# A hybrid RWKV-7 and short-convolution block on one core: a later issue time for the store of the solved diagonal blocks, an earlier priority for the Gram masks and the weights' casts

## The chip, the core and the metric

The kernel runs on one core of a Trainium2 chip. The metric is the device time of one execution in microseconds (us). Three executions of the kernel before took 1057.23, 1058.88 and 1059.51 us; their median, 1058.88 us, is the number that the change is measured against. Engines are named as in the profile: PE is the matrix engine (PEld its weight loads), DVE, ACT and POOL are the vector, scalar and GpSimd engines, and SP is the queue from which nearly all DMAs are issued.

## What is computed

One layer of a streaming encoder: 16 meta tokens and 512 tokens, width 2048, are normalised and multiplied by one input matrix with 8320 columns. Half of the columns feed 16 heads of RWKV-7 time mixing, the other half a gated convolution of width 3. Both results pass one output projection, are added to the residual and are normalised. Cut to what matters here:

```python
hn = _rmsnorm(h_res, norm_in_g); P = hn @ w_in          # columns: r, k, v, g, low rank | B, C, h, gate
# per head, per token:  sa = S kk;  S = S*w - sa b^T + v k^T;  y = S r
y = _rwkv7_recurrence(r, decay, k, v, kk, kk * a)
y_a = (groupnorm(y) + bonus) * silu(g_r)
y_b = Bg * _causal_depthwise_conv(Cg * hc, conv_w) * silu(g_c)
out = _rmsnorm(h_res + concat([y_a, y_b]) @ w_out)
```

## The kernel before

**Projection.** The input weights come in tiles of 128 columns of the matrix ("units": `k2`, `r2`, `v2`, `g2` and so on, in the order of `plan`, lines 105 to 110). A unit is two loads of 512 KB, `wr<j>` (L134), with j counted over the whole stream. Each load is cut into two quarters of 512 columns, and each quarter is split in two float32r parts: ACT copies it to `wh` (L126), and DVE (first quarter of a load) or POOL (second quarter) subtracts to get `wl` (L127). PE then runs three products per step: `wh` with `xh`, `wh` with `xl`, `wl` with `xh` (L315). There are three raw buffers for `wr` and six for each of `wh` and `wl`; a load is issued when both quarters of the load three places earlier are split.

**Recurrence in chunks of 64 tokens.** For every pair of heads i (0 to 7), `prepare(i)` (L569) makes decayed keys and queries on DVE and ACT; PE forms Gram matrices of them (L625) and DVE masks these into `gt` (`masked`, L632 to L639). There are two Gram passes for each i. The second one reuses the PSUM banks of the first: chunk 8 takes the banks of `zc`, the 16 transposes of the keys (L654) take those of `za`, so PE can't begin it before the masks of the first pass have been read out. The masked matrices then go to DRAM (`sg`, L688; `opd`, L567), the 16 by 16 diagonal blocks come back as `d` (L696), and DVE inverts them by doubling (L700 to L733) into `y`. Then

- `sx <- y` (L748) stores the solved blocks, and `load_inverse` (L737) reads them back as `xT` and `xo` in the layout of heads (four DMAs, L739 and L740);
- `y` has one buffer: POOL's clearing of `y` for the next i (L699) waits until that store has read it.

`invert` (L771) takes two such i at a time (0 and 1, 2 and 3, 4 and 5, 6 and 7); it begins with a transpose of `xT` (L784). After all pairs comes `recur`, and then the output projection (L1069).

**What sets the order.** PE's instructions stand in the order in which the program lists them: the projection is a generator, and `fill(ns)` puts about that many ns of it between two steps of the recurrence. DVE, ACT, POOL and SP are ordered by a scheduler from priorities, and each then works strictly through its own list. `tc.high_priority(offset)` moves instructions forward in priority: `AHEAD` is used for results that PE waits for, `WEIGHTS` for the casts of the weights. `later(ns, fn)` (L482) puts a DMA off until that much projection time has been listed, and `run_pending` (L486) then lists it behind the last weight load:

```python
def run_pending(upto):
    while pending and pending[0][0] <= upto:
        fn = pending.pop(0)[1]
        with tc.issue_after(state["dma"]):
            fn()
```

Of the kernel before, what the change touches and what calls it, by code (L numbers as in the profile page):

```python
# [13 lines left out]
ALU = mybir.AluOpType  # L14
# [4 lines left out]
P = 128  # L19
# [26 lines left out]
)  # L46


AHEAD, WEIGHTS = 3000, 1500


def _constants():
# [24 lines left out]
def hymba_kernel(ctx: ExitStack, tc: tile.TileContext, xt, xtok, w_in, w_out, pv, lup, cst, msk, gf, out):  # L77
    nc = tc.nc
# [11 lines left out]
    gmask = cs[:, C_GM : C_GM + 256].rearrange("p (h c) -> p h c", h=2)  # L90
# [6 lines left out]
    def col(off, i=0):  # L97
        return pvt[:, off + i : off + i + 1]
# [183 lines left out]
    for b in range(2):  # L282
# [5 lines left out]
        out=omm, in0=pvt[:, V_MU : V_MU + 33], scalar1=-1.0, scalar2=1.0, op0=ALU.mult, op1=ALU.add  # L288
    )
    for d, off in (  # L290
# [4 lines left out]
            out=d, in0=pvt[:, off : off + 8], scalar1=0.5, scalar2=None, op0=ALU.mult  # L295
        )
    nc.vector.tensor_scalar(
        out=hv[:, 4], in0=pvt[:, V_KA : V_KA + 8], scalar1=-0.5, scalar2=1.0, op0=ALU.mult, op1=ALU.add
# [183 lines left out]
    def later(ns, fn):  # L482
        pending.append((clock[0] + ns, fn))
        pending.sort(key=lambda e: e[0])
# [48 lines left out]
    def ahead():  # L533
        return tc.high_priority(offset=AHEAD)

    def c3(t):
        return t.rearrange("p (c s) -> p c s", s=CH)
# [31 lines left out]
    def prepare(i):  # L569
        p = i % 2  # L570
# [21 lines left out]
            out=bk[:, :, 0], in0=c3(k), scalar=hv[:, 2, i : i + 1], in1=c3(te), op0=ALU.mult, op1=ALU.mult  # L592
# [3 lines left out]
            out=ta, in0=ta, scalar1=hv[:, 3, i : i + 1], scalar2=hv[:, 4, i : i + 1], op0=ALU.mult, op1=ALU.add  # L596
        )
        nc.vector.scalar_tensor_tensor(
            out=ar[:, :, 0], in0=c3(k), scalar=col(V_KK, i), in1=e1[:, :, 0:CH], op0=ALU.mult, op1=ALU.mult
# [8 lines left out]
            out=ar[:, 1:NCH, 1], in0=c3(r), in1=e1[:, 1:NCH, 1 : CH + 1], op=ALU.mult  # L608
        )
        nc.vector.scalar_tensor_tensor(  # L610
            out=r, in0=r, scalar=hv[:, 5, i : i + 1], in1=ta[:, CH:LP], op0=ALU.mult, op1=ALU.mult
# [8 lines left out]
        gt = cq.tile([P, 2, NCH, P], F32, tag=f"gt{p}", name=f"gt{i}")  # L620
# [9 lines left out]
                )  # L630

        def masked(z, c0, c1):  # L632
            for h in range(2):
                nc.vector.tensor_tensor(
                    out=gt[:, h, c0:c1],
                    in0=z[h],
                    in1=gmask[:, h].unsqueeze(1).to_broadcast([P, c1 - c0, P]),
                    op=ALU.mult,
                )  # L639


        za = [pz.tile([P, 4, P], F32, tag="tz", name=f"g{i}_0_{h}") for h in range(2)]
# [1 line left out]
        for c in range(8):  # L644
            gram(za if c < 4 else zc, c, c // 4 * 4)
        masked(za, 0, 4)
        masked(zc, 4, 8)
        fill(FW["gram2"])
        ze = [pi.tile([P, 1, P], F32, tag=("misc", "ser")[h], name=f"g{i}_8_{h}") for h in range(2)]
        zz = [pz.tile([P, NCH - 1, CH], F32, tag="tz", name=f"bt{i}_{h}") for h in range(2)]  # L650
        gram(ze, 8, 8)
        for c in range(NCH - 1):
            for h, hs, ho in heads:
                nc.tensor.transpose(  # L654
                    zz[h][:, c], bk[hs, c, h : h + 2, :].rearrange("p a s -> p (a s)"),
                    ident[hs, 64 * h : 64 * h + 64],
                )
        masked(ze, 8, 9)
        for h in range(2):
            nc.scalar.copy(bt[:, h], zz[h])  # L660
        fill(FW["gram3"])
        n2 = tr(f"n2{i}")
        for j, (a, b) in enumerate(((0, 288), (288, LP))):
            z = pi.tile([2, b - a], F32, tag=("misc", "ser")[j], name=f"n2_{i}_{a}")
# [11 lines left out]
        sx = scr_x[i % 2]  # L676
# [4 lines left out]
        def blocks(t):  # L681
            return bass.AP(tensor=t.tensor, offset=t.offset, ap=[[BLK, 8 * NCH], [CH, 16], [1, 16]])
# [15 lines left out]
        y = cq.tile([NB, 256], F32, tag="y", name=f"y{i}").rearrange("p (s t) -> p s t", t=16)  # L698
# [11 lines left out]
        def sub(x, r0, c0, dims):  # L710
            return bass.AP(tensor=x.tensor, offset=x.offset + r0 * 16 + c0, ap=[list(x.ap[0])] + dims)

        for m in (2, 4, 8):
            for b in range(16 // (2 * m)):
# [4 lines left out]
                    out=pq,  # L719
                    in0=sub(d, o, o + m, [[16, m], [0, m], [1, m]]),  # L720
                    in1=sub(y, o + m, o + m, [[0, m], [1, m], [16, m]]),
                    op=ALU.mult,
                )
                nc.vector.tensor_reduce(
                    out=tq.rearrange("p (i j) -> p i j", i=m), in_=pq, op=ALU.add, axis=AX.X
                )
                nc.vector.tensor_tensor(
                    out=pq,
                    in0=sub(y, o, o, [[16, m], [0, m], [1, m]]),
                    in1=bass.AP(tensor=tq.tensor, offset=tq.offset, ap=[list(tq.ap[0]), [0, m], [1, m], [m, m]]),  # L730
                    op=ALU.mult,
# [13 lines left out]
                    ),  # L745
                )

        later(12500, lambda: nc.sync.dma_start(blocks(sx), y))  # L748
        later(15500, load_inverse)

        for h, hs, ho in heads:
            stash(i, bt[hs, h], O_B, CH, 64 * h, 64, 0, NCH - 1)
# [241 lines left out]
    for i in range(0, NPAIR, 2):  # L994
        invert([prepare(i), prepare(i + 1)])
# [160 lines left out]
    with tc.manual_schedule(engines={mybir.EngineType.DVE, mybir.EngineType.Activation, mybir.EngineType.Pool}):  # L1156
# [9 lines left out]
        for part in range(2):  # L1166
# [3 lines left out]
            if part == 0:  # L1170
                finish(2)
                nc.vector.tensor_tensor(
                    out=fv[:, 3, 0:1], in0=fv[:, 3, 0:1], in1=ssq[:, 3, 3:4], op=ALU.add
# [60 lines left out]
```

## Time and profile before

| | us |
|---|---|
| executions, median of 3 (lowest to highest) | 1058.88 (1057.23 to 1059.51) |
| profiled execution | 1061.95 |
| its span, first to last instruction | 1060.1 |
| time of PE matmuls within the span | 1039.8 (98%) |
| DVE / ACT / POOL busy | 560.8 / 365.4 / 305.0 |

The profiled execution is 3.07 us above the median of the others, and 1.85 us of it lie outside the span. Matmuls are pipelined and the profile models their ends, so a row's duration (0.28 us for 128x258) is longer than the distance from one start to the next (0.12 us); waits are best read from starts. In a timeline each row is start, duration, engine, line, operation, out<-in, shape and count, and in brackets the idle time before it with what ended it. In a list of waits a row is who waited for whom, then the total, the number of times and the longest, in us. In a table of windows, a row is a stretch of time, its length, the busy time of each engine, the granted clock of PE (1.00 is full speed), the mean share of the DMA engines and GB/s.

### The profile page before, as it was taken

To read this page: it belongs to the slowest core of one execution; us is meant where nothing else is said; L and a number is where in the kernel's file an instruction comes from. 1 tells how busy PE (TensorE), PEld (TensorE's weight loads), DVE (VectorE), ACT (ScalarE), POOL (GpSimd) and SP (SyncE) were. 2 spreads that over 40 slices of the span, in tenths; PEclk is the share of its full clock that TensorE was granted. 3 is DMA by queue.
4 is the path that set the end of the run, shared out by engine and by line. 5 is a ranking of instruction groups with operands and counts; after the bars stand their busy time and mean duration, and the time that the engine had idled before them with its cause. 6 is when DMAs were issued, how large, how long until landed. Compare 5 with 4: busy or idle time off the path is not lost.

```text
span 1060.1 us, 23983 instructions
## 1 busy us (share of the span) xinstructions
PE 1039.8 (98%) x9973; PEld 948.8 (89%) x9973; DVE 560.8 (53%) x1072; ACT 365.4 (34%) x682; POOL 305.0 (29%) x315
## 2 busy tenths in 40 slices
PE   8999999999999999999999999999999999999996
PEld 6999997999998999998999989888798988888885
DVE  6774865558563657563767643354544672212132
ACT  6553422433332433233443332222222342323232
POOL 0132413323232323132332231322323241424232
PEclk9999999999999999999999999999999999999999
DMA  8446474464843364654366648777653879223324
GB/s 290 139 121 158 115 177 141 111 151 105 223 134 115 110 164 115 167 150 117 102 150 157 137 150 275 244 210 239 190 151 90 273 222 331 85 94 100 100 60 159
DMA packets 182893, 167.49 MB, mean 158 GB/s; under 512 B 120960, under 2 KB 143232, under 8 KB 182400
## 3 DMA queue, kind: packets, MB, share of 16 engines
q1 hardware_dynamic: 182208, 164.90, 54.0%
q8 instruction: 78, 1.28, 0.5%
q10 hardware_dynamic: 576, 1.07, 0.3%
q14 instruction: 31, 0.25, 0.1%
HBM read 129.05 MB, written 36.88 MB: 157 GB/s over the span
## 4 chain that ended last, share of the span: by engine, by line
PE 86%; DVE 6%; DMA 3%; issue 2%; POOL 2%; ACT 1%; SPq 0%; DVEq 0%; ACTq 0%; POOLq 0%
PE o L1069 17%; PE ps_C L315 9%; PE ps_gc L315 9%; PE ps_k L315 9%; PE ps_B L315 8%; PE ps_h L315 8%; PE ps_g L315 6%; PE ps_r L315 6%; PE ps_v L315 6%; DMA wr<-in_w_in_dram 2%; PE zs L940 1%; PE g L625 1%; DMA wq<-in_w_in_dram 1%; PE ps_lora L315 1%; PE rz L888 1%
## 5 line engine op out<-in xcount | busy, mean ns | idle before, releaser
L127 POOL TENSOR_TENSOR wl<-wr,wh 128x512 fp32r<-128x512 f32 x150 | 207.7, 1385 | 470.2 <-ACT wh L126 440.7
L126 ACT CAST wh<-wr 128x512 fp32r<-128x512 f32 x312 | 188.7, 619 | 391.6 <-PE o L1069 94.0
L127 DVE TENSOR_TENSOR wl<-wr,wh 128x512 fp32r<-128x512 f32 x162 | 126.1, 783 | 250.9 <-ACT wh L126 240.9
L1069 PE MATMUL o<-wh,m 128*128 128x512 f32 (+1 forms) x484 | 145.3, 384 | 0.0
L1069 PEld LDWEIGHTS o<-wh,m 128*128 128x128 f32 x484 | 89.6, 188 | 21.3
L1069 PE MATMUL o<-wl,m 128*128 128x512 f32 (+1 forms) x242 | 92.6, 389 | 0.0
L315 PE MATMUL ps_g<-xh,wl 128*128 128x258 f32 (+1 forms) x256 | 72.9, 285 | 0.9 <-DVE wl L127 0.8
L315 PE MATMUL ps_h<-xh,wl 128*128 128x258 f32 (+1 forms) x256 | 73.6, 288 | 0.0
L315 PE MATMUL ps_g<-xl,wh 128*128 128x258 f32 (+1 forms) x256 | 73.2, 286 | 0.0
L315 PE MATMUL ps_k<-xl,wh 128*128 128x264 f32 x256 | 73.1, 286 | 0.0
L315 PE MATMUL ps_v<-xh,wh 128*128 128x264 f32 x256 | 73.1, 286 | 0.0
L315 PE MATMUL ps_g<-xh,wh 128*128 128x258 f32 (+1 forms) x256 | 73.0, 285 | 0.0
L315 PE MATMUL ps_h<-xh,wh 128*128 128x258 f32 (+1 forms) x256 | 73.0, 285 | 0.0
L315 PE MATMUL ps_k<-xh,wh 128*128 128x264 f32 x256 | 72.9, 285 | 0.0
L315 PE MATMUL ps_h<-xl,wh 128*128 128x258 f32 (+1 forms) x256 | 72.8, 284 | 0.0
L315 PE MATMUL ps_k<-xh,wl 128*128 128x264 f32 x256 | 72.7, 284 | 0.0
L315 PE MATMUL ps_r<-xh,wh 128*128 128x258 f32 (+1 forms) x256 | 72.2, 282 | 0.5 <-ACT wh L225 0.5
L315 PE MATMUL ps_v<-xh,wl 128*128 128x264 f32 x256 | 72.7, 284 | 0.0
L315 PE MATMUL ps_v<-xl,wh 128*128 128x264 f32 x256 | 72.7, 284 | 0.0
L315 PE MATMUL ps_C<-xh,wh 128*128 128x258 f32 (+1 forms) x256 | 72.3, 282 | 0.0
L315 PE MATMUL ps_C<-xh,wl 128*128 128x258 f32 (+1 forms) x256 | 72.3, 282 | 0.0
L315 PE MATMUL ps_r<-xl,wh 128*128 128x258 f32 (+1 forms) x256 | 72.1, 282 | 0.0
(271 smaller groups left out, 2705.3 us busy)
## 6 DMA issues: line engine op xcount, KB each, us to landing
wr<-in_w_in_dram SPq DMA_DIRECT2D x127, 512.0 KB
ct<-opd SPq DMA_DIRECT2D x64, 288.0 KB
wr<-in_w_out_dram SPq DMA_DIRECT2D x32, 512.0 KB
opd<-ar SPq DMA_DIRECT2D x8, 576.0 KB
opd<-gt SPq DMA_DIRECT2D x16, 288.0 KB
opd<-bt SPq DMA_DIRECT2D x32, 128.0 KB
xres<-in_xtok_dram SPq DMA_DIRECT2D x4, 768.0 KB
out_dram<-xres SPq DMA_DIRECT2D x6, 512.0 KB
```

Source lines behind the costliest of these rows:

```text
L126: nc.scalar.copy(hi, rq)
L127: eng.tensor_tensor(out=lo, in0=rq, in1=hi.bitcast(F32), op=ALU.subtract)
L315: nc.tensor.matmul(ps[r], ww[:, w], xx[:, kt, a:b], start=(kt == 0 and n == 0), stop=(kt == KT - 1 and n == 2))
L625: nc.tensor.matmul(z[h][:, c - c0], bk[hs, c, h : h + 2, :].rearrange("p a s -> p (a s)"), ar[hs, c].rearrange("p a s -> p (a s)"), start= ...
L888: nc.tensor.matmul(z[e][ho if e else hs, 0, k], t[hs, o : o + CH], t[hs, O_V : O_V + CH] if part else st[hs, 4 * e + k], start=(part == 0 ...
L940: nc.tensor.matmul(d[hs, j], t[hs, o : o + CH], x[hs], start=(a == 0), stop=(a == b - 1))
L1069: nc.tensor.matmul(ps[t + p], mm[:, tk], ww[:, o], start=(jj == 0 and q == 0), stop=(jj == KT - 1 and q == 2))
```

## The change

Three edits. The store `sx <- y` and its read-back are put off by more projection time (p is i % 2); the masks of the Gram matrices get the priority of `AHEAD`; and both priority offsets are doubled.

```diff
-AHEAD, WEIGHTS = 3000, 1500
+AHEAD, WEIGHTS = 6000, 3000
...
         def masked(z, c0, c1):
-            for h in range(2):
-                nc.vector.tensor_tensor(
-                    out=gt[:, h, c0:c1],
-                    in0=z[h],
-                    in1=gmask[:, h].unsqueeze(1).to_broadcast([P, c1 - c0, P]),
-                    op=ALU.mult,
-                )
+            with ahead():
+                for h in range(2):
+                    nc.vector.tensor_tensor(
+                        out=gt[:, h, c0:c1],
+                        in0=z[h],
+                        in1=gmask[:, h].unsqueeze(1).to_broadcast([P, c1 - c0, P]),
+                        op=ALU.mult,
+                    )
...
-        later(12500, lambda: nc.sync.dma_start(blocks(sx), y))
-        later(15500, load_inverse)
+        later(13500 if p else 29000, lambda: nc.sync.dma_start(blocks(sx), y))
+        later(16500 if p else 33000, load_inverse)
```

What the two built programs' lists show, engine by engine, for the whole kernel:

- PE and ACT: the same instructions in the same order.
- DVE: the masks stand where they stood. In i = 3, 5 and 7 one split of a weight quarter (`wl80`, `wl128`, `wl176`) changes places with the second half of the PSUM read-out `pr_v` (L334). Nothing else moves.
- POOL: in i = 3, 5 and 7 the clearing of `y` moves behind two weight splits.
- SP, i = 2, 4 and 6 (the one that is solved while its partner is prepared): see the lists below for i = 2; 4 and 6 are the same with other numbers.
- SP, i = 0: the store of the gate `gated0` moves in front of the four read-backs. SP, odd i: nothing moves.

```
SP before: wr39, sx<-y2, wr40, wr41, xT2 xo2 xT2 xo2, wr42, wr43, opd<-ar3, opd<-vs3, wr44, ...
SP after:  wr39, wr40, opd<-ar3, wr41, wr42, sx<-y2, wr43, opd<-vs3, xT2 xo2 xT2 xo2, wr44, ...
```

## The prediction

> **What bounds the kernel now.** I read the page first, then who PE waited for.
>
> ```profile
> span 1060.1 us, 23983 instructions
> PE 1039.8 (98%) x9973; PEld 948.8 (89%) x9973; DVE 560.8 (53%) x1072; ACT 365.4 (34%) x682; POOL 305.0 (29%) x315
> ```
>
> PE is busy for 1039.8 of 1060.1 us and the change leaves its list of instructions alone. So nothing can be won but the waits between PE's instructions, and there are few. The list of PE's waits, its largest rows outside the first 25 us:
>
> ```profile
> PE rz L940 <- issue: 2.0, 1, 2.0
> PE g L625 <- DVE gt L634: 1.5, 3, 0.9
> PE ps_B L315 <- DVE wl L127: 1.4, 1, 1.4
> PE ps_g L315 <- DVE wl L127: 0.8, 2, 0.4
> ```
>
> The second row names what this change is about: three times the second Gram pass (L625) waits for DVE's masks (L634). These are i = 3, 5 and 7. The true price is read from starts in PE's timeline: from the last projection matmul before that pass to the first one after it. First i = 1, where nothing waits, then 3, 5 and 7.
>
> ```profile
> 128.31 0.28 PE L315 MATMUL ps_C<-xh,wl 128*128 128x258 f32 x1
> ...
> 129.44 0.39 PE L315 MATMUL ps_C<-xh,wh 128*128 128x258 f32 x1
> ```
> ```profile
> 267.93 0.28 PE L315 MATMUL ps_g<-xh,wl 128*128 128x256 f32 x1
> ...
> 269.90 0.39 PE L315 MATMUL ps_g<-xh,wh 128*128 128x256 f32 x1
> ```
> ```profile
> 421.60 0.28 PE L315 MATMUL ps_g<-xh,wl 128*128 128x256 f32 x1
> ...
> 424.32 0.39 PE L315 MATMUL ps_g<-xh,wh 128*128 128x256 f32 x1
> ```
> ```profile
> 577.08 0.28 PE L315 MATMUL ps_g<-xh,wl 128*128 128x256 f32 x1
> ...
> 579.24 0.39 PE L315 MATMUL ps_g<-xh,wh 128*128 128x256 f32 x1
> ```
>
> The same work takes 1.13 us at i = 1, and 1.97, 2.72 and 2.16 us at i = 3, 5 and 7 (the last three fences, in this order). The excess is 0.84 + 1.59 + 1.03 = **3.46 us**. That is the whole sum which the masks can give back.
>
> Why are the masks late? The chain of waits, cut to the stretch around i = 5:
>
> ```profile
> 413.18 6.34 DMA wr<-in_w_in_dram
> ...
> 419.62 0.63 ACT wh L126
> ...
> 420.27 0.69 DVE wl L127
> 420.97 2.40 DVE gt L634 x4
> ```
>
> The masks stand behind a weight split (`wl130`, of the load `wr65`) in DVE's list, and that load took 6.34 us to land. The whole chain has the same link for the other two:
>
> ```profile
> 259.52 5.58 DMA wr<-in_w_in_dram
> ```
> ```profile
> 568.74 5.70 DMA wr<-in_w_in_dram
> ```
>
> Why did it take so long? SP's list of waits, and SP's timeline:
>
> ```profile
> SPq L748 <- DVE y L733: 73.3, 6, 16.4
> ```
> ```profile
> 410.24 0.32 SPq L748 DMA_DIRECT2D sx<-y  x1
> 410.65 0.60 SPq L134 DMA_DIRECT2D wr<-in_w_in_dram  x1
> ```
> ```profile
> 413.62 0.60 SPq L739 DMA_DIRECT2D xT<-sx  x1
> ```
>
> SP stood still, up to 16.4 us, until DVE had solved `y4`. Everything behind the store was then issued in a bunch: `wr64` at 410.65, `wr65` at 413.18 (the chain's row), four read-backs from 413.62. `wr65` shared the DMA engines with all of them.
>
> **The change, part by part.**
>
> *The masks' priority: nothing.* DVE's built list has the masks where they were, still behind `wl130`. No instruction is added or removed on any engine. The doubled offsets move only one split past half a PSUM read-out in i = 3, 5 and 7, and nothing on ACT. The wait `ps_g <- wl`, 0.8 us, should therefore stay: the casts it needs stand on ACT behind this row, which waits for DVE.
>
> ```profile
> 408.52 0.62 ACT L551 CAST rk_h<-r 128x512 fp32r<-128x512 f32 x1 [3.80 <-DVE r L610]
> ```
>
> *The later store: this is the working part.* For i = 2, 4 and 6 SP now issues `wr40`, the store of `ar3` (`opd<-ar`), `wr41` and `wr42` ahead of `sx <- y2` (numbers of i = 2). I follow i = 4, where they are `wr64`, `ar5`, `wr65`, `wr66`, `y4`.
>
> ```profile
> 393.68 1.28 POOL L127 TENSOR_TENSOR wl<-wr,wh 128x512 fp32r<-128x512 f32 x1 [0.33 <-ACT wh L126]
> ```
> ```profile
> 410.26 2.90 POOL L127 TENSOR_TENSOR wl<-wr,wh 128x512 fp32r<-128x512 f32 x1 [2.85 <-ACT wh L126]
> ```
> ```profile
> 406.49 0.68 DVE L607 TENSOR_TENSOR ar<-r,e 128x512 f32<-128x512 f32 x1
> ```
> ```profile
> 414.99 1.14 ACT L126 CAST wh<-wr 128x512 fp32r<-128x512 f32 x2 [3.77 <-DMA wr<-in_w_in_dram]
> ```
>
> 1. `wr64` needs the buffer that POOL's split frees at 393.68 + 1.28 = 394.96. It goes out there, some 15.7 us earlier than 410.65.
> 2. `opd<-ar` waits for DVE until 406.49 + 0.68 = 407.17. It holds `wr65` behind it, which costs nothing: `wr65` needs the buffer of `wr62`, which POOL's split frees only at 410.26 + 2.90 = 413.16. So `wr65` is still issued at about 413.2, 6.0 us after `ar5` is ready.
> 3. What changes is its company. `wr64` and `ar5` have landed; `wr66` and the store follow behind it; the read-backs come later still. For its time to landing I take `wr64` of the trace before, the nearest row: issued at 410.65, its cast starts at 414.99, so 4.34 us, with another load 2.5 us behind it. The other end is 6.34, as slow as before.
> 4. At 4.34 us the cast starts at 417.52 instead of 419.62, 2.10 us earlier. ACT and DVE are free by then, since the casts of `wr64`, for which `sh_v` and the rest of `v5` had waited, are no longer late. So the masks come 2.10 us earlier too; they end at 420.97 + 2.40 - 2.10 = 421.27, before PE leaves the projection at 421.60. PE lost 1.59 us there: the wait is gone, with 0.5 us to spare. For i = 3 and 7 the load took 5.58 and 5.70; on the same footing the masks come 1.3 and 1.5 us earlier, against 0.84 and 1.03 us lost, and again about 0.5 us is left.
>
> So the point of decision is a landing time of about 4.8 us: below it the three excesses vanish, at 6.3 none does.
>
> *What else moves, at nothing.* POOL's clearing of `y` now waits for a store that lands later, but stands behind two splits; the split behind it is for a weight quarter that PE reaches more than one unit later (a unit is 96 matmuls of 0.12 us, 11.5 us). If that cover were gone, PE would wait for `wl` as at `ps_B`, 1.4 us. The four read-backs are listed behind `opd<-vs` and land a few us later; `invert` of that pair comes only behind the odd i and another 22.5 us of projection (`fill(FW["solve"])`). `gated0` at i = 0 passes four read-backs that wait for the store anyway. The odd i keep their order. Bounds for each: 0 to 1.4 us lost, and I take 0.
>
> *Sum.* 1061.95 - 3.46 = 1058.49 on the profiled execution's scale; that execution lies 3.07 above the median, so the median comes to 1058.88 - 3.46 = **1055.4 us**.
>
> **A rule against the row: the clock.** The table of windows, at `ps_B` and at i = 5:
>
> ```profile
> 158.51:161.92 3.41, 1.97 (x9) 1.30 (x8) 3.41 (x3) 1.98 (x4) 3.41 (x4) 1.00 0.28 44
> ```
> ```profile
> 161.92:165.33 3.41, 3.41 (x17) 2.75 (x16) 2.24 (x3) 0.62 (x1) 1.46 (x1) 1.00 0.96 254
> ```
> ```profile
> 421.34:424.75 3.41, 2.36 (x28) 1.90 (x27) 2.58 (x6) 0.37 (x1) 0.79 (x1) 1.00 1.07 359
> 424.75:428.17 3.42, 3.42 (x18) 3.42 (x17) 1.12 (x2) 1.26 (x3) 0.16 (x1) 0.50 1.11 308
> ```
>
> Behind the longest of the three waits PE ran for 3.42 us at half clock: 18 matmuls, where 0.12 us each would allow 28. That cost between 10 x 0.12 = 1.2 and half of 3.42 = 1.7 us; I take 1.5. Behind `ps_B`, with less PE work in the window, the clock stayed at 1.00.
>
> The Trainium skill, page "TensorE: Matmul & The Clock Gate", section "HAM oscillation — how this bites in real kernels", gives as its rule that PE should have no idle gap above about 3.4 us. By it a gap of 0.9 us costs no clock, and removing it would give the 3.46 us alone; the row at 424.75 speaks against that, the one at 161.92 for it.
>
> **Rivals.**
>
> - *The half clock goes too.* If the executions that are timed have this stretch as the profiled one has, its 1.5 us go with the wait: 1058.88 - 4.96 = 1053.9. For it: the row. Against: it followed one wait of several, and the median may not hold it.
> - *The change doesn't do what it says.* The masks did not move in DVE's list, so all hangs on one landing time. If `wr65` still takes 5 to 6 us, because `wr66` and the store are now close behind it, PE waits as before: 1058.9. For it: loads in company took 5.58 to 6.34. Against: `wr64` also had a load close behind and took 4.34.
> - *A new wait on SP (slower).* The store, and with it the read-backs and `wr44`, go out later and push the stores of the odd partner's matrices. Before, SP still waited for ACT there, at least this long (i = 7):
>
> ```profile
> SPq L684 <- ACT n L667: 0.8, 1, 0.8
> ```
>
> A delay of SP above 0.8 us moves the odd solve on DVE, and what stands behind it there, by as much. Its price is that of `ps_B`, where weight splits queued behind the solve of i = 1: 1.4 us each in three pairs, 4.2. With the masks' gain that is 1058.88 - 3.46 + 4.2 = 1059.6; with a half clock behind one of them 1061.1, behind all three 1064.1; from one on it counts as slower. How late SP will be, the trace before can't show: the four read-backs, 0.60 us each to issue, move behind `opd<-vs`, 2.4 us, while two weight loads and `opd<-ar` move out of the way ahead of it. It may come out on either side of 0.8.
>
> **How the numbers follow.** The full gain without the clock 0.50 (1055.4); with the clock 0.19 (1053.9); nothing 0.15 (1058.9); the new wait 0.16 (1059.6 to 1064.1). The range takes in the first three with 0.7 us of scatter: 1053.2 to 1059.6. About 0.2%, 2.1 us, is what a measurement of this kernel can tell from no change; that is below 1056.8 or above 1061.0. Faster: 0.47 of the first case, all of the second: 0.66. Slower: the part of the new wait that has a half clock, 0.12. Within: the rest, 0.22.
>
> **What would show it.** Right: PE's waits have no row `g <- gt`; the passages at i = 3, 5 and 7 take 1.13 us; SP's wait `L748 <- y` loses some 45 us and `L567 <- ar` gains most of them; `ps_g <- wl` stays near 0.8; no half clock around i = 5. Wrong: a load in front of the masks still takes over 4.8 us, `wl` waits appear at i = 4 to 7 in the stretch of `invert`, or the gain is smaller than the excess that vanished, which would mean that PE gives it back later.

## The result and the profile after

| | us |
|---|---|
| before, median (lowest to highest) | 1058.2 (1056.29 to 1062.32) |
| after, median (lowest to highest) | 1055.59 (1054.37 to 1059.71) |
| ratio, 95% interval | 0.9976, 0.9966 to 0.9986 |
| after, profiled execution / its span | 1055.68 / 1053.9 |

After is 2.5 us faster by the ratio (1.5 to 3.6); 3.46 was forecast. The same program, timed twice more below (e1, e5), gave 0.9995 and 0.9983. All three together, weighted by their intervals, say 0.9984 or about 1.6 us. e1 alone can't be told from no change, and it lies further from the first timing than their intervals make likely. So a gain is probable, and it is smaller than the first figure.

The page's head and the list of PE's waits, of after:

```profile
span 1053.9 us, 23986 instructions
PE 1035.8 (98%) x9973; PEld 945.8 (90%) x9973; DVE 565.4 (54%) x1072; ACT 366.3 (35%) x682; POOL 307.8 (29%) x315
```
```profile
PE rz L941 <- issue: 1.6, 1, 1.6
...
PE zy L945 <- issue: 1.3, 1, 1.3
...
PE ps_B L315 <- DVE wl L127: 0.9, 1, 0.9
...
PE ps_g L315 <- DVE wl L127: 0.8, 2, 0.4
```

The row `g <- gt` is gone from the list. But a list by releaser shows only waits that the profile can assign. The starts in PE's timeline show that a part of the wait is still there at i = 3 and 5 (first and second pair of rows), and nothing at i = 7:

```profile
266.97 0.28 PE L315 MATMUL ps_g<-xh,wl 128*128 128x256 f32 x1
...
268.43 0.39 PE L315 MATMUL ps_g<-xh,wh 128*128 128x256 f32 x1
...
420.14 0.28 PE L315 MATMUL ps_g<-xh,wl 128*128 128x256 f32 x1
...
421.71 0.38 PE L315 MATMUL ps_g<-xh,wh 128*128 128x256 f32 x1
...
573.11 0.28 PE L315 MATMUL ps_g<-xh,wl 128*128 128x256 f32 x1
...
574.25 0.38 PE L315 MATMUL ps_g<-xh,wh 128*128 128x256 f32 x1
```

The passages take 1.46, 1.57 and 1.13 us, so 0.33 + 0.44 = 0.77 us is left of the 3.46, in this execution. Why? Three views of after around i = 5: POOL, SP (`wr65`, then the moved store), then ACT and DVE.

```profile
408.80 3.85 POOL L127 TENSOR_TENSOR wl<-wr,wh 128x512 fp32r<-128x512 f32 x1 [2.85 <-ACT wh L126]
```
```profile
412.67 0.33 SPq L134 DMA_DIRECT2D wr<-in_w_in_dram  x1
414.27 0.39 SPq L749 DMA_DIRECT2D sx<-y  x1
```
```profile
417.01 0.62 ACT L126 CAST wh<-wr 128x512 fp32r<-128x512 f32 x1 [4.34 <-DMA wr<-in_w_in_dram]
```
```profile
410.82 0.68 DVE L127 TENSOR_TENSOR wl<-wr,wh 128x512 fp32r<-128x512 f32 x1
...
417.66 0.69 DVE L127 TENSOR_TENSOR wl<-wr,wh 128x512 fp32r<-128x512 f32 x1 [1.20 <-ACT wh L126]
418.27 2.89 DVE L635 TENSOR_TENSOR gt<-g,cs 128x512 f32<-128x512 f32 x5
```

The load ahead of the masks is cast 4.34 us after its issue, the very time that was forecast; that it fits so well is luck, since the landing scatters by 1.7 us from load to load (below). But POOL's split that frees its buffer takes 3.85 us, where before it took 2.90. That split starts 421.60 - 410.26 = 11.34 us before PE leaves the projection in before, and 420.14 - 408.80 = 11.34 in after; so the load now goes out 420.14 - 412.67 = 7.47 us before that point, where before it was 421.60 - 413.18 = 8.42. The time that can be hidden shrank by 0.95 us. New beside POOL's split is the DVE split at 410.82 (`wl128`): its load `wr64` now lands early enough for DVE to reach it there.

SP's list of waits, of after:

```profile
SPq L567 <- DVE ar L607: 46.6, 7, 11.8
...
SPq L749 <- DVE y L734: 20.2, 3, 7.9
```
```profile
SPq L740 <- DMA sx<-y: 11.8, 5, 4.1
SPq L685 <- ACT n L668: 7.8, 4, 2.2
```

The wait for `y` fell from 73.3 to 20.2 us, and the wait for `ar` grew from 11.4 to 46.6, as forecast. The four waits for `n` in this row are those of even i. At i = 3, 5 and 7, where the late store could do harm, SP's store of `n` still waits for ACT; the profile puts these waits down to other instructions of ACT:

```profile
SPq L685 <- ACT th_r L361: 0.7, 1, 0.7
```
```profile
SPq L685 <- ACT wh L126: 0.6, 1, 0.6
```
```profile
SPq L685 <- ACT th_r L361: 0.5, 1, 0.5
```

In before they were 1.3, 2.7 and 0.8 us. They are shorter but not gone, so the late store does not hold up the odd solve there. The clock is next. Windows of after around i = 5 and around the wait of `rz`:

```profile
420.97:424.39 3.42, 3.42 (x40) 3.35 (x40) 1.60 (x4) 1.64 (x3) 1.64 (x3) 1.00 0.35 80
424.39:427.80 3.41, 3.41 (x29) 3.14 (x28) 1.80 (x3) 2.37 (x6) 1.29 (x1) 1.00 0.84 212
728.16:731.57 3.41, 1.92 (x27) 1.85 (x27) 2.33 (x6) 0.00 (x0) 0.00 (x0) 1.00 1.02 360
731.57:734.98 3.41, 3.41 (x23) 3.02 (x22) 1.62 (x4) 1.25 (x2) 1.46 (x3) 1.00 0.87 301
```

No half clock at either place; the profiled execution of before had one at both (its other one was at 735.37). The two spans differ by 6.2 us, of which about 3 are the two half clocks, at the prediction's 1.5 each: profiled spans alone would overstate this change more than twofold.

### The profile page after: what moved, and what is told of

Same layout as the page of the kernel before. It is cut to its first block, busy times and chain, and to the rows that moved or that the text cites. A ratio compares the mean times of both kernels' runs of the same rounds, so it can differ in the third digit from the quotient of the medians.

```text
span 1053.9 us, 23986 instructions
## 1 busy us (share of the span) xinstructions
PE 1035.8 (98%) x9973; PEld 945.8 (90%) x9973; DVE 565.4 (54%) x1072; ACT 366.3 (35%) x682; POOL 307.8 (29%) x315
## 3 DMA queue, kind: packets, MB, share of 16 engines
q8 instruction: 78, 1.28, 0.5%
## 4 chain that ended last, share of the span: by engine, by line
PE 91%; DVE 4%; issue 2%; DMA 1%; ACT 1%; POOL 1%; SPq 0%; DVEq 0%; ACTq 0%; POOLq 0%
PE o L1070 17%; PE ps_g L315 9%; PE ps_C L315 9%; PE ps_gc L315 9%; PE ps_k L315 9%; PE ps_B L315 8%; PE ps_h L315 8%; PE ps_r L315 7%; PE ps_v L315 7%; PE g L625 2%; PE zs L941 1%; PE rz L889 1%; PE ps_lora L315 1%; PE zy L945 1%; DMA wq<-in_w_in_dram 1%
## 5 line engine op out<-in xcount | busy, mean ns | idle before, releaser
L127 POOL TENSOR_TENSOR wl<-wr,wh 128x512 fp32r<-128x512 f32 x150 | 210.4, 1405 | 458.0 <-ACT wh L126 428.0
```

Of the source, the lines that this page charges most:

```text
L127: eng.tensor_tensor(out=lo, in0=rq, in1=hi.bitcast(F32), op=ALU.subtract)
```

## The experiments

Gains are 1058 us times one minus the ratio, against before on the same chip. Where "landing" is given, it is from the issue of `wr41`, `wr65`, `wr89` on SP to their last part in memory, for i = 3, 5, 7.

**e1: the two `later` lines alone.**

```diff
 # kernel before
-        later(12500, lambda: nc.sync.dma_start(blocks(sx), y))
-        later(15500, load_inverse)
+        later(13500 if p else 29000, lambda: nc.sync.dma_start(blocks(sx), y))
+        later(16500 if p else 33000, load_inverse)
```

> The kernel before with the two later() lines of the change alone; the masks stay outside ahead() and the offsets stay at 3000 and 1500. Theory (the moved store and read-backs are the whole change): the lists of every engine come out as after, so the ratio to before is near 0.9976 (2.6 us gained), the second Gram pass takes about 1.46, 1.57 and 1.13 us at i = 3, 5 and 7, and POOL's split ahead of the late load takes about 3.85 us. Rival (the priority edits do part of it): the gain differs from after's by more than 1 us, or the masks start later than after's.

Ratio 0.9995 (0.9984 to 1.0005). Every engine's list is that of after, as expected, so this is the same program; the edits of priority do nothing. But the expected 2.6 us did not come, and the passages took 2.72, 1.29 and 2.22 us. The chain of waits, PE's and DVE's rows at i = 3:

```profile
259.09 5.32 DMA wr<-in_w_in_dram
...
565.94 4.83 DMA wr<-in_w_in_dram
```
```profile
266.49 0.28 PE L315 MATMUL ps_g<-xh,wl 128*128 128x256 f32 x1
267.70 0.97 PE L625 MATMUL g<-ar,bk 64*128 64x128 f32 x3 [0.93 <-DVE gt L634]
...
269.20 0.39 PE L315 MATMUL ps_g<-xh,wh 128*128 128x256 f32 x1
```

The loads landed in 5.32, 3.88 and 4.83 us, where the profiled execution of after had 4.13, 4.24 and 3.77. With the load issued 7.4 us ahead, each of the six passages fits landing minus 3.75 us (5.32 - 3.75 = 1.57; measured 1.59). The point of decision is 3.75, not 4.8, and the landing time scatters across it.

**e2: the read-backs alone.**

```diff
 # kernel before
-        later(15500, load_inverse)
+        later(16500 if p else 33000, load_inverse)
```

> The kernel before with load_inverse alone moved to 16500 (odd pair) or 33000 (even pair): SP still stands at the store of y, up to some 16 us, and wr40, wr64, wr88 still go out late, but three of the four read-backs no longer follow directly behind wr41, wr65, wr89. Theory (the load is slow because of the transfers in its company): it lands in 4.2 to 4.9 us instead of 5.58 to 6.34, the passages fall to 1.1 to 1.5 us, 2.5 to 3.5 us gained. Rival (it is slow because SP stood and the load ahead of it is late): it lands in 5.5 us or more, the passages stay near 1.97, 2.72 and 2.16, gain below 0.7 us.

Ratio 0.9998 (0.9988 to 1.0008): the expectation missed, for the edit does less than it was meant to. Only one load (`wr42` at i = 3) passes the four read-backs. SP of e2 at i = 3, the late load with the one behind it, then the first and the last read-back:

```profile
258.96 1.81 SPq L134 DMA_DIRECT2D wr<-in_w_in_dram  x2
260.89 0.60 SPq L739 DMA_DIRECT2D xT<-sx  x1
...
263.67 0.63 SPq L740 DMA_DIRECT2D xo<-sx  x1
```

The read-backs start 1.9 us behind the late load instead of 0.4, and all of them still within its landing time. The landings were 5.32, 4.67 and 5.43, the passages 1.75, 1.45 and 1.86. The mean landing, 5.14, is 0.4 below that of before's order on SP (5.51 over e3, e6, e10 and before), which three landings can't tell from their scatter, and far above the 4.33 of after's order (after, e1, e4, e5, e7). So it stays open what in the late load's company slows it. Besides the read-backs there is the load ahead (`wr40`, `wr64`, `wr88`), which the store of `y` holds up here as in before, and which lands 1.5 to 1.8 us after the late load has gone out. Neither was taken away by itself.

At i = 5 the load landed in 4.67 us, and PE still lost 0.32. DVE's split started only at 418.15, behind the transpose of `v` (`vs`, L761), which began at 417.45; in after that transpose is over at 416.46 and the split waits for its load. So the earlier `wr64` is needed there too, as step 4 of the prediction has it.

**e3 and e4: the split held back behind the masks**, on before and on after.

```diff
-        eng.tensor_tensor(out=lo, in0=rq, in1=hi.bitcast(F32), op=ALU.subtract)
+        def low():
+            eng.tensor_tensor(out=lo, in0=rq, in1=hi.bitcast(F32), op=ALU.subtract)
+        held.append(low) if q in (82, 130, 178) else low()
...
         masked(zc, 4, 8)
+        while held:
+            held.pop(0)()
```

> The kernel before with DVE's half of the weight splits of quarters 82, 130 and 178 (the subtract that gives wl) emitted behind the masks of the second Gram pass; nothing else. The loads stay as slow as before. Theory (the masks are late only because that split stands ahead of them on DVE): all three passages fall to 1.13 us and 3.46 us are gained (5.0 if the half clock goes too); no row g <- gt. Rival (the masks wait for something else that is late too, such as the first part of that pass or the load itself through ACT): the passages stay above 1.5 us and less than 1 us is gained.

> The kernel after with the same three splits held back behind the masks. Theory (what is left of the wait in after, 0.33 us at i = 3 and 0.44 us at i = 5, is the same queue on DVE): passages 1.13 us at all three, and 0.8 us faster than after, 3.4 us faster than before. Rival (the rest is something else, or the later start of that wl costs PE as much further on): the rest stays, or a new row of ps_g or ps_B waiting for wl takes 0.5 us or more, and the time is that of after or above.

All six passages are 1.12 us: the masks wait for that split and for nothing else. But e3's ratio is 0.9996 (0.9986 to 1.0005), e4's 0.9977 (0.9967 to 0.9988). A new row in PE's list says where a part went; of e3, then of e4:

```profile
PE ps_h L323 <- DVE wl L130: 0.9, 3, 0.4
```
```profile
PE ps_h L323 <- DVE wl L130: 0.7, 2, 0.4
```

Holding the split also moved later loads in SP's list, and 28 us on a projection waits for their splits. There one matmul starts 0.57, 0.48 and 0.64 us behind the one ahead of it (0.35, 0.63 and 0.64 in e4), where 0.12 is usual, and the next one 0.22. Together this takes back 1.6 us in e3 and in e4. A half clock sat behind the wait of `rz` in both profiles. So both fall short of what was expected (3.46 and 3.4 us); e6 and e7 make the same test without these waits.

**e5: after, a second time.** No edit.

> The kernel after, unchanged, a second time; e1 is the same program but for line numbers, and gave 0.9995 where after gave 0.9976. Theory (one gain of about 2 us, that two sets of 12 to 22 runs with landing times of 3.8 to 5.4 us for the load scatter around): ratio 0.997 to 0.999 and passages between those of after (1.46, 1.57, 1.13) and of e1 (2.72, 1.29, 2.22). Rival (the gain belongs to the set of runs in which after was first timed): ratio 0.9992 or more. Rival (the lines differ after all between e1 and after): 0.9976 again, with passages below 1.6.

Ratio 0.9983 (0.9971 to 0.9994); landings 5.50, 3.79, 4.15, passages 2.86, 1.18, 1.56. The ratio lies between those of after and e1, as the first theory had it. The passages scatter further than it had them: 2.86 is above both at i = 3, 1.18 below both at i = 5.

**e6 and e7: the two halves of that load changed over**, on before and on after.

```diff
-   nc.gpsimd if q and j > 8 else nc.vector
+   nc.gpsimd if ((q and j > 8) != (j in (41, 65, 89))) else nc.vector
```

> The kernel before with the two halves of the loads wr41, wr65, wr89 changed over: POOL splits wl82, wl130, wl178 and DVE splits wl83, wl131, wl179, which stand behind the masks in DVE's list; nothing else moves on any engine. Theory (the masks wait for nothing but that split, and each us of wait that goes is a us gained): passages 1.13 us at all three, 3.46 us gained without the waits that e3 brought in at ps_h, ratio 0.9967, or 0.9953 where a half clock goes too. Rival (PE gives it back further on, as the time of e3 could be read): passages 1.13 and a ratio above 0.9985, with new waits of 2 us or more in PE's list.

> The kernel after with the same halves changed over. Theory (what is left in after is the same split with a load that lands in 3.8 to 5.4 us): passages 1.13 us, and 0.8 (by the profile of after) to 2.9 us (by that of e1) faster than after. Rival (nothing is left): the time of after, within 0.5 us.

Passages 1.12 to 1.13 in all six, no new row above 0.2 us in PE's list. e6: 0.9979 (0.9970 to 0.9987), 2.2 us gained (1.4 to 3.2). e7: 0.9974 (0.9963 to 0.9985), 2.7 us. So one line takes the whole wait out of before with no change to SP, and is worth 2.2 us, not 3.46. The landings under e6 say why: 5.40, 5.03 and 5.72 would have cost 0.7 + 0.3 + 1.0 = 2.0 us, by landing minus 4.7. e7 lies 0.9 us below e5, within both intervals, so the times don't show whether it adds anything to after.

**e8: e7, and ACT's cast `rk_h` behind four casts of weights.**

```diff
 # kernel of e7, prepare()
-        rh, rl = split(r, f"rk{i}", SEQ)
+        if not (p and i > 1):
+            rh, rl = split(r, f"rk{i}", SEQ)
...
+        if p and i > 1:
+            with tc.issue_after(casts[79 + 24 * (i - 3)]):   # casts[q]: ACT's cast wh<q>
+                rh, rl = split(r, f"rk{i}", SEQ)
```

> e7, and ACT's cast rk_h of i = 3, 5 and 7 moved behind the casts wh76 to wh79 (wh124 to wh127, wh172 to wh175), for which ps_g waits 0.8 us in before and after. Theory (those casts are late only because rk_h, which waits for DVE's r, stands ahead of them): the row ps_g <- wl goes or falls below 0.2, 0.6 to 1.4 us faster than e7; ratio to before 0.994 to 0.996. Rival (rk_h so late makes the zb matmuls or a buffer late, or the casts wait for their loads): a new row of PE's waits of 0.5 us or more and the time of e7 or above.

Ratio 0.9982 (0.9973 to 0.9991): missed, slower than e7 by 0.8 if anything. The casts came early, as meant. The two waits of the row `ps_g <- wl`, at i = 3 and 5, fell from 0.4 to 0.2 us each, so `rk_h` was a part of their cause. But at i = 7 a wait of 0.2 us became 1.1, and the row grew to 1.6 us in all. DVE, POOL and PE at i = 7:

```profile
559.98 2.25 DVE L734 TENSOR_TENSOR prod<-y,tt 72x512 f32<-72x512 f32 x1
...
562.87 1.28 DVE L129 TENSOR_TENSOR wl<-wr,wh 128x512 fp32r<-128x512 f32 x2
```
```profile
556.99 4.21 POOL L129 TENSOR_TENSOR wl<-wr,wh 128x512 fp32r<-128x512 f32 x2 [4.39 <-ACT wh L128]
```
```profile
563.60 0.39 PE L317 MATMUL ps_g<-xh,wl 128*128 128x258 f32 x1 [1.09 <-DVE wl L129]
```

POOL's splits now start while DVE solves `y6`; a step of the solve takes 2.25 us where it takes 1.18 at i = 3, and PE waits for the DVE split behind it.

**e9: `wl80`, `wl128`, `wl176` on POOL**, on after.

```diff
-   nc.gpsimd if q and j > 8 else nc.vector
+   nc.gpsimd if (q and j > 8) or j in (40, 64, 88) else nc.vector
```

> The kernel after with wl80, wl128 and wl176 (first halves of wr40, wr64, wr88) split by POOL instead of DVE; nothing else moves. Theory (POOL's split of wl79, wl127, wl175, which frees the buffer for wr41, wr65, wr89, takes 3.85 us in after because DVE now splits wl80 beside it, and 2.90 without): 2.9 to 3.2 us, the load is issued about 8.4 us before the end of the projection instead of 7.4, and 4.7 us of landing time are hidden instead of 3.75; with landings of 3.8 to 5.5 us the three excesses together come to 0 to 1 us, 1 to 2 us faster than after. Rival (the split is as long for another reason): it stays near 3.85, the load at 7.4, the time that of after.

This is the test of the failed step, and it holds. POOL, SP and PE of e9 at i = 5:

```profile
408.13 2.90 POOL L127 TENSOR_TENSOR wl<-wr,wh 128x512 fp32r<-128x512 f32 x1 [2.85 <-ACT wh L126]
```
```profile
411.06 0.33 SPq L134 DMA_DIRECT2D wr<-in_w_in_dram  x1
```
```profile
419.48 0.28 PE L315 MATMUL ps_g<-xh,wl 128*128 128x256 f32 x1
...
420.60 0.38 PE L315 MATMUL ps_g<-xh,wh 128*128 128x256 f32 x1
```

The split is back at 2.90, the load goes out 419.48 - 411.06 = 8.42 us ahead, the landings are 4.07, 3.68 and 3.68, all passages 1.12 to 1.13. Ratio 0.9980 (0.9971 to 0.9989), 2.1 us. The mechanism is shown by the length of the split and the time of the issue. The passages alone say little, since a point of decision of 3.75 us would have hidden two of these three landings as well. Whether the time beats that of after can't be told from the intervals.

**e10: the two edits of priority alone**, the `later` lines as in before.

```diff
 # kernel before, and masked() under ahead() as in the change
-AHEAD, WEIGHTS = 3000, 1500
+AHEAD, WEIGHTS = 6000, 3000
```

> The kernel before with the masks inside ahead() and the offsets doubled, the store and the read-backs where they were. Theory (no list changes on any engine, so it is a second look at before): ratio 1.000 within 0.001; the load takes 5.0 to 5.8 us, as in e3 and e6 which have its order on SP, so that the three excesses come to about 2.5 us and not to the 3.46 of the first profile. Rival (the priorities do part of it): ratio 0.999 or less and shorter passages at the same landing times.

Ratio 1.000 (0.9989 to 1.0011), every list as in before. Landings 5.25, 5.46, 5.49; passages 1.68, 1.90 and 1.94: 2.13 us of excess, where the profiled execution of before had 3.46. At i = 5:

```profile
420.08 0.28 PE L315 MATMUL ps_g<-xh,wl 128*128 128x256 f32 x1
421.97 0.39 PE L315 MATMUL ps_g<-xh,wh 128*128 128x256 f32 x1
```

**e11: e7 and e9 together** (DVE keeps only the second half of `wr41`, `wr65`, `wr89`; POOL takes both halves of `wr40`, `wr64`, `wr88`).

> The edits of e7 and e9 together. Theory (once the masks no longer stand behind the split, an earlier load gives nothing more on PE): passages 1.13 us and the time of e7 within 0.5 us. Rival (the earlier load, or less work beside POOL, also shortens the waits of ps_g): 0.5 us or more faster than e7, ps_g <- wl below 0.5.

Ratio 0.9978 (0.9968 to 0.9989), `ps_g <- wl` still 0.8: nothing beyond e7 that can be measured, as the theory had it.

**e12: a fourth buffer for the weight loads**, on after.

```diff
-   raw = wp.tile([P, 1024], F32, tag="raw", name=f"wr{j}", bufs=3)
+   raw = wp.tile([P, 1024], F32, tag="raw", name=f"wr{j}", bufs=4)
```

> The kernel after with four buffers for the weight loads instead of three; many loads move ahead in SP's list, and some splits on DVE and ACT. Theory (a load waits for the buffer that a late split frees, and masks, ps_g and ps_B wait for loads that are late): rows g <- gt, ps_B <- wl and ps_g <- wl go, 1.5 to 3 us faster than after; ratio to before 0.995 to 0.997. Rival (the splits then come up in front of other work on DVE and ACT): new rows of PE's waits and the time of after or above.

Ratio 0.9952 (0.9939 to 0.9965): 5.1 us faster than before (3.7 to 6.5), better than anything above. PE's whole list of waits of 0.6 us and more outside the first 25 us is now

```profile
PE rz L941 <- issue: 1.8, 1, 1.8
...
PE zy L945 <- issue: 1.0, 1, 1.0
```

`g <- gt`, `ps_g <- wl` and `ps_B <- wl` are all gone. The loads waited for buffers, and with one more they are early. Some splits on DVE and ACT stand elsewhere too, so that for `ps_B` and `ps_g` this cause is argued, not shown by itself. By the profiles with before's order the rows that went are worth about 2.4 us (the masks, worked out in the next section), 1.1 (`ps_B`) and 0.8 (`ps_g`), 4.3 in all, which lies within the interval of the gain. The buffer was tried on after only, in five executions.

## Why the prediction was right, and where it was not

- **What bounds the kernel, and the mechanism: right.** Only PE's waits could be won; the masks were late through the split ahead of them (e3, e6), and that split through its load. Moving the store and its read-backs brought the landing from 5.51 to 4.33 us on average, over 12 and 15 loads. That this is through the company they kept with the load was the prediction's reason; which of them slowed it is not shown (e2). The forecast 4.34, counted to the cast and so 0.1 us longer, came from one row of another load; that it hit the mean so closely is partly luck.
- **"The masks' priority: nothing": right** (e1, e10). **"The doubled offsets move only one split": wrong.** `wl80`, `wl128` and `wl176` change places through the `later` lines (e1 has it, e10 has not).
- **The step that failed: "about 0.5 us is left", a point of decision of 4.8 us** (counted to the cast; 4.7 to the landing). It took POOL's split at 2.90 us from before. DVE's `wl128`, brought forward by the load that now lands early, runs beside that split and stretches it to 3.85. The decision point became 3.75, in the middle of landings of 3.77 to 5.50, and the wait vanishes in some passages and stays in others; e5 still had 1.73 us at i = 3. Taking `wl128` off DVE restores 2.90 and hides the load (e9). The prediction saw that very split move and priced it at nothing.
- **The second mis-sized term: 3.46.** It was summed from one execution, and that one was 3.07 us above the median. Four profiles with before's order on SP have landings of 4.99 to 6.34 us, mean 5.51; by landing minus 4.7 that is 3 x 0.8 = 2.4 us per execution. Removing all of it gained 2.2 (e6).
- **Why the forecast time came out all the same.** The measured median, 1055.59, is close to the forecast 1055.4 in part because before's median over 22 executions is 1058.2 and not 1058.88. Both errors make the gain of the masks smaller than forecast, and something that the prediction leaves out adds to it: the wait at `ps_B` was 1.44 us in before, 0.9 to 1.1 in e3, e6 and e10, and 0.3 or 0.9 in after, e1, e4, e5 and e7, about 0.5 us less on average. The masks give 2.4 - 1.9 = 0.5 us (1.9: the mean of 0.77, 2.84 and 2.21 in after, e1 and e5). Together 1 us is accounted for, of the 1.6 that three timings give, and the rest is open; 2.5 in the first of them was on the lucky side. What shortens `ps_B` was not tried; the one move on SP at i = 0 is a candidate, though e2, which has it, still shows 0.9.
- **The clock.** The half clock at i = 5 is absent from all other profiles, those with waits as long too: the passage of 2.72 us at i = 3 of e1 lies across two of the windows, with the border at 267.63, and the clock stayed at 1.00. As a rival it had a chance of 0.19 on the strength of one row.
- **The new wait on SP: did not come.** SP still waits for ACT at i = 3, 5 and 7, and no `wl` wait appeared around `invert`. `ps_g <- wl` stayed at 0.8, as forecast; moving the cast that was blamed for it halved its two waits and brought a longer one elsewhere (e8).

## What to carry to other kernels

A wait's price taken from one profile is one draw: where a DMA's landing time decides, compare it over several profiles of the same order of issue before summing. When work comes earlier, ask whom it now runs beside: the step that frees the next buffer may grow by more than the slack that was won. And before moving transfers about a late load, see what its issue waits for; here one more buffer, on top of the reordering, took the gain from about 1.6 to 5.1 us.

## What the hardware showed that was not expected

- POOL's split and DVE's steps on two SBUF tiles take turns rather than run side by side. In before, a tiny step of DVE's solve (72x8) takes 0.16 us, and 1.20 when POOL's split, at 393.68 for 1.28 us, runs:

```profile
393.00 0.16 DVE L727 TENSOR_TENSOR prod<-y,tt 72x8 f32<-72x8 f32 x1
...
393.78 1.20 DVE L727 TENSOR_TENSOR prod<-y,tt 72x8 f32<-72x8 f32 x1
```

  And POOL's split, 1.28 us there, takes 2.90 beside a run of DVE's splits, and 3.85 when one more split of 0.68 us follows, though a read-out of PSUM stands between. The run of before, at i = 5:

```profile
410.73 1.28 DVE L127 TENSOR_TENSOR wl<-wr,wh 128x512 fp32r<-128x512 f32 x2
```

  In before, after and e9 POOL's split ends about 1.15 us after the last of DVE's splits does (412.01 to 413.16, 411.50 to 412.65, 409.89 to 411.03), nearly its own 1.28. So it seems to wait for all of them, while the read-outs of 0.4 us behind them run beside it. The Trainium skill, page "SBUF — State Buffer", section "Who interferes with whom", has a rule for it: a DVE instruction with two inputs in SBUF contends with a GpSimd instruction that reads SBUF, and the order of issue decides which of the two is blocked. The rows of 0.16 and 1.20 us agree. That POOL's split lets several splits of DVE pass, also one behind a read-out, is what the rows of after add, and what the forecast's 2.90 did not allow for.
- One load of one program, with the same neighbours on SP, lands in very different times. In after, e1 and e5 `wr41` took 4.13, 5.32 and 5.50 us, and `wr89` 3.77, 4.83 and 4.15. What decides it stays open.
- The half clock comes in stretches of 3.41 us on a fixed grid: those of before start at 21.98, 424.75 and 735.37 us, 118 and 91 times 3.413 us apart. The window ahead does not settle by PE's busy time whether one comes. Behind the wait of `rz`, e3 (first two rows) and e1 (last two) differ by 0.01 us in the window ahead, and only e3 has the half clock. Nor does the number of matmuls, 22 and 93 here, for in before a half clock followed a window with 76 (731.95 to 735.37, PE busy for 1.40 us). What decides it stays open.

```profile
728.75:732.16 3.41, 1.54 (x22) 1.47 (x23) 1.93 (x5) 0.00 (x0) 0.00 (x0) 1.00 1.02 377
732.16:735.57 3.41, 3.41 (x17) 3.35 (x16) 1.76 (x5) 0.94 (x2) 0.20 (x1) 0.50 0.84 279
```
```profile
728.43:731.84 3.41, 1.53 (x93) 1.43 (x84) 1.38 (x2) 0.00 (x0) 0.00 (x0) 1.00 0.90 292
731.84:735.25 3.41, 3.41 (x31) 3.25 (x28) 2.90 (x7) 1.12 (x2) 0.20 (x1) 1.00 1.01 341
```
